# The first stage of a fused SSM, attention and FFN block: low parts by half tiles, spread products in banks of their own, another load order, the last tile's vector on ScalarE

## The chip, the cores and the metric

The kernel runs on one core of a Trainium2 chip. A core has engines that each run their own list of instructions in order and wait for one another by semaphores: TensorE (PE, matrix products into PSUM), VectorE (DVE), ScalarE (ACT), GpSimd (POOL), and SyncE (SP), which here issues the DMA transfers. The metric is the device time of one execution in microseconds, lower is better.

## The reference

The block takes x of 512 tokens by 1024 features. What the edited stage computes is the beginning of it, and a small product that is needed only at the end:

```python
n1 = rmsnorm(h, g_mix[i])                      # x * rsqrt(mean(x*x) + eps) * g_mix
z = n1 @ w_in[i]                               # SSM input, queries, keys and values, gates, merge gates
...
lam = lax.complex(jnp.minimum(a_re, -1e-4), a_im); dt = jnp.exp(log_dt)
a_bar = jnp.exp(lam * dt)                      # modulus rho, angle a_im * dt
...
h = h + gate * (p[i] @ w_ple_proj[i])          # the "embedding" product
```

Between the first and the last lines stand a diagonal state space mixer, an attention with three branches, a merge, and a feed-forward part with a short convolution. They are unchanged.

## The kernel before

Every product is made in three passes of a fast 32-bit format. A number is split in a high part (a copy on ACT that rounds) and a low part (the number less its high part, a subtraction on DVE or POOL); high times high, high times low and low times high are added up in one PSUM bank. `copy` (line 74) is the ACT copy, `tt` (line 53) the subtraction, `mm3` (line 81) the three products. PSUM has eight banks here, in four tags of two: "acc", "s", "t" and "o". A tile that asks for a bank of a tag waits until the reader of the tile that had it before is done. `either()` gives "o" and "acc" in turn.

The order of the first stage is written out by hand for PE, ACT, DVE and POOL (lines 444 to 528): within it each engine runs its instructions as written. Instructions from outside it, and everything after it, are ordered by a planner that simulates the engines' time; it may slip single ones in between (two copies from line 622 and two from line 623 stand in ACT's list in the middle of the stage). `issue_after` keeps some of them behind a named instruction.

The tokens are four tiles of 128 (qt 0 to 3), the features eight slices of 128 (k). The stage does this:

- `embedded(i, qt)`: the product of p with `w_ple_proj`, column half i, token tile qt, two slices by three passes; six products of 512 columns. `embedded_out` copies the bank to memory on ACT, from where SP stores it to DRAM (line 533). The weight halves are loaded in two parts each by `wpload` and split into `wp`.
- `squared` (ACT) sums the squares of a token tile's row form; `rooted` (POOL) makes the reciprocal root of it; `spread` (PE) multiplies it with a scaled identity, so that every partition holds it along the 128 tokens (`rb`, in a bank of tag "s").
- `x_scaled(qt, half)`: DVE multiplies four slices of the transposed x with the column `gmix` and with `rb`, one instruction per slice. `n_high` is the ACT copy of the half, `n_low` the DVE subtraction for the whole tile. They give `n1h` and `n1l`.
- `v_passes(qt, passes)`: three passes of eight products of 280 columns, high by high, low by high, high by low, with the value weights `WV`, in a bank that `either()` gives. The bank that tile 2 gets is the one from which `embedded_out(1, 2)` reads; tile 3's is that of `embedded_out(1, 3)`. `v_high` and `v_low` take gates and values out.
- `u_split(ct, 0)` and `u_split(ct, 1)` are the two parts of the split of the first two weight tiles for the projections.
- `some(n)` runs the next n steps of `angles()` (line 390), small DVE operations on 128x16: steps 1 to 15 end with dt, step 16 is lr = lre * dt, and the following ones make the angles' coarse and fine parts. `some(16)` stands early, `some(50)`, which means all that is left, near the end.

Behind the stage come the projections (`proj`, line 202): 24 products of 512 columns each, with a weight tile that is loaded, copied (high) and subtracted (low). Beside them DVE makes sines and cosines (lines 549 to 578) and POOL makes rho = exp(lr) (line 545), which may start once tile 0's gates are done on POOL; from them come the powers, the input matrix `bb` and its products `z` on DVE, and tables on POOL.

Of the kernel before, what the change touches and what calls it, by code (L numbers as in the profile page):

```python
# [12 lines left out]
AF = mybir.ActivationFunctionType  # L13
# [3 lines left out]
MUL, ADD, SUB = ALU.mult, ALU.add, ALU.subtract  # L17

P = 128
T = 512  # L20
NQ = T // P
D = 1024
KD = D // P
# [21 lines left out]
def hybrid_kernel(ctx: ExitStack, tc: tile.TileContext, A, out):  # L45
    nc = tc.nc
    V, G, S, PE = nc.vector, nc.gpsimd, nc.scalar, nc.tensor

    def dr(name, off, ap):
        t = A[name]  # L50
        return bass.AP(tensor=t.tensor, offset=t.offset + off, ap=ap)

    def tt(o, a, b, op, e=V):
        e.tensor_tensor(o, a, b, op=op)  # L54
# [7 lines left out]
    def stt(o, a, s, b, op0, op1, e=V):  # L62
        e.scalar_tensor_tensor(o, a, s, b, op0=op0, op1=op1)  # L63
# [10 lines left out]
    def copy(o, a):  # L74
        S.activation(o, a, AF.Copy)  # L75
# [24 lines left out]
    def bank(tag, name):  # L100
        return psp.tile([P, 512], F32, tag=tag, name=name, bufs=BANKS[tag])

    def slot(p, tag, shape, dt, name):
        return p.tile(shape, dt, tag=tag, name=name, bufs=1)
# [104 lines left out]
    n1h = slot(pn, "nh", [P, KD, T], F32R, "n1h")  # L209
    n1l = slot(pn, "nl", [P, KD, T], F32R, "n1l")  # L210
# [14 lines left out]
    gmix, gains, dcol, prm, pes, cvp = (cols[:, a:b] for a, b in zip(COLS, COLS[1:]))  # L225
# [7 lines left out]
    xT = slot(cp, "h16", [P, NQ, KD, P], F32, "xT")  # L233
    wv0 = slot(py, "y8", [P, 2, KD, P], F32, "wv0")
    rows = [wv0[:, 1].rearrange("p a b -> p (a b)"), *(px.tile([P, D], F32, name=f"row{qt}") for qt in range(1, NQ))]
    root = px.tile([P, P], F32, name="root")
    ts(root, ident, math.sqrt(D), None, MUL, None, G)
    half = px.tile([P, 1], F32, name="half")
    G.memset(half, -0.5)

    def rowload(qt):
        nc.sync.dma_start(rows[qt], dr("x", qt * P * D, [[D, P], [1, D]]))

    def xload(qt):
        nc.sync.dma_start(xT[:, qt], dr("x_t", qt * P * D, [[D, P], [P, KD], [1, P]]))
# [4 lines left out]
    wpr = slot(pa, "v8", [P, 2, 2, 512], F32, "wpr")  # L250
    wp = [slot(*t, [P, 2, 2, 512], F32R, f"wp{i}") for i, t in enumerate(((pS, "Uc"), (pa, "ptc")))]
    pjd = pud.tile([2, NQ, P, 512], F32, name="pjd")

    def wpload(i, k):
        nc.sync.dma_start(wpr[:, i, k], dr("w_ple_proj", (2 * i + k) * T * P, [[T, P], [1, T]]))
# [2 lines left out]
        nc.sync.dma_start(pin[:, k], dr("p_t", k * T * P, [[T, P], [1, T]]))  # L258
        wpload(0, k)
    nc.sync.dma_start(cols, dr("cols", 0, [[NCOLS, P], [1, NCOLS]]))  # L260
    for qt in range(2):
        rowload(qt)
    for k in range(2):
        wpload(1, k)
    xload(0)
    VV = slot(pa, "v8", [P, NQ, 2, 2, 2, HD], F32R, "VV")
    gates = pa.tile([P, NQ, 24], F32, name="gates")
    WV = slot(pa, "kv", [P, 2, KD, 280], F32R, "WV")
# [13 lines left out]
    def wv(x, i):  # L282
        w0, w, raw = VCOLS[i]
        return WV[:, x, :, w0:w0 + w], raw
# [13 lines left out]
    def v_high(qt):  # L298
        S.activation(gates[:, qt], vps[qt][:, 256:280], AF.Tanh, scale=0.5)
        x, hi, _ = v_parts(qt)  # L300
        copy(hi, x)
        ts(gates[:, qt], gates[:, qt], 0.5, 0.5, MUL, ADD, G)
# [9 lines left out]
    def squared(qt):  # L312
        S.activation(rows[qt], rows[qt], AF.Square, accum_out=ss4[:, qt:qt + 1])

    rbp, rx = {}, {}

    def rooted(qt):

        r = rx[qt] = small("rx")
        ts(r, ss4[:, qt:qt + 1], D * EPS, None, ADD, None, G)  # L320
        tt(r, r, half, ALU.pow, G)

    def spread(qt):
        if not rbp:
            rbp[0] = bank("s", "rb")
        PE.matmul(rbp[0][:, qt * P:(qt + 1) * P], rx[qt].to_broadcast([P, P]), root, start=True, stop=True)

    def x_scaled(qt, half):
        for k in range(4 * half, 4 * half + 4):
            stt(xT[:, qt, k], xT[:, qt, k], gmix[:, k:k + 1], rbp[0][:, qt * P:(qt + 1) * P], MUL, MUL)  # L330

    def n_of(qt, half):
        ks = slice(4 * half, 4 * half + 4)
        return (slice(None), ks, slice(qt * P, qt * P + P)), xT[:, qt, ks]

    def n_high(qt, half):
        o, x = n_of(qt, half)
        copy(n1h[o], x)

    def n_low(qt):  # L340
        o = (slice(None), slice(None), slice(qt * P, qt * P + P))
        tt(n1l[o], xT[:, qt], n1h[o], SUB)

    def normed_tile(qt):
        for half in range(2):
            x_scaled(qt, half)
            n_high(qt, half)

    uw = []

    def u_split(ct, part):
        if not part:
            uw.append([pw.tile([P, KD * P], F32R, name=n, tag=n).rearrange("p (k c) -> p k c", k=KD)
                       for n in ("wh", "wl")])
            copy(uw[ct][0], uraw[ct])
        else:
            tt(uw[ct][1], uraw[ct], uw[ct][0], SUB)
# [67 lines left out]
    def embedded(i, qt, passes=range(3), ks=range(2)):  # L425
        if (i, qt) not in pjb:
            pjb[i, qt] = bank("t" if i and qt < 2 else either(), "pje")
        for k in ks:
            for n in passes:
                PE.matmul(pjb[i, qt], pT[int(n == 1)][:, k, qt * P:(qt + 1) * P], wp[i][:, int(n == 2), k], start=n + k == 0,  # L430
                          stop=n + k == 3)

    def embedded_out(i, qt):
        n = 4 * i + qt
        if n == 0:
            pjs.append(slot(pa, "v4", [P, 2, 512], F32, "pjs0"))
            pjs.append(wv0[:, 1].rearrange("p (k a) b -> p k (a b)", k=2))
        elif n == 4:
            t = slot(pS, "Uc", [P, 4, 512], F32, "pjs2")
            pjs.extend((t[:, :2], t[:, 2:]))  # L440
        pjo[i, qt] = pjs[n // 2][:, n % 2]
        copy(pjo[i, qt], pjb[i, qt])

    with tc.manual_schedule(engines={mybir.EngineType.PE, mybir.EngineType.Activation, mybir.EngineType.DVE,
                                    mybir.EngineType.Pool}):
        warm = bank("s", "warm")
        for _ in range(6):
            PE.matmul(warm[:, :P], ident, root, start=True, stop=True)
        angled = angles()

        def some(n):
            for _ in range(n):
                next(angled, None)

        for k in range(2):
            copy(pT[0][:, k], pin[:, k])
            copy(wp[0][:, 0, k], wpr[:, 0, k])
            tt(pT[1][:, k], pin[:, k], pT[0][:, k], SUB)
            tt(wp[0][:, 1, k], wpr[:, 0, k], wp[0][:, 0, k], SUB)
        squared(0)  # L460
        for k in range(2):
            for n in range(3):
                for qt in range(NQ):
                    embedded(0, qt, (n,), (k,))
        rooted(0)
        some(16)
        squared(1)
        rooted(1)
        for k in range(2):
            copy(wp[1][:, 0, k], wpr[:, 1, k])  # L470
            tt(wp[1][:, 1, k], wpr[:, 1, k], wp[1][:, 0, k], SUB)
        for qt in range(2):
            embedded_out(0, qt)
        embedded(1, 0)
        spread(0)
        embedded(1, 1)
        x_scaled(0, 0)
        n_high(0, 0)
        embedded_out(0, 2)
        x_scaled(0, 1)  # L480
        n_high(0, 1)
        embedded_out(0, 3)
        embedded(1, 2)
        n_low(0)
        copy(*wv(0, 0))
        wv_lo(0)
        copy(*wv(0, 1))
        wv_lo(1)
        embedded(1, 3)
        for qt in range(2):  # L490
            embedded_out(1, qt)
        spread(1)
        v_passes(0, (0, 1))
        squared(2)
        rooted(2)
        normed_tile(1)
        v_passes(0, (2,))
        n_low(1)
        for qt in (2, 3):
            embedded_out(1, qt)  # L500
        spread(2)
        v_passes(1, (0,))
        squared(3)
        rooted(3)
        normed_tile(2)
        v_passes(1, (1, 2))
        n_low(2)
        v_high(0)
        u_split(0, 0)
        exp_at = last(mybir.EngineType.Pool)  # L510
        spread(3)
        v_passes(2, (0,))
        normed_tile(3)
        v_passes(2, (1, 2))
        n_low(3)
        v_high(1)
        v_low(0)
        v_low(1)
        u_split(0, 1)
        some(50)  # L520
        trig_at = last(mybir.EngineType.DVE)
        u_split(1, 0)
        v_passes(3, (0, 1, 2))
        for qt in (2, 3):
            v_high(qt)
            v_low(qt)
        zero_at = last(mybir.EngineType.Activation)
        u_split(1, 1)
# [117 lines left out]
    for lv in range(5):  # L646
        n = 1 << lv
        m = MID + n
        rotate([t[:, :, m:m + n] for t in tab], [t[:, :, MID:m] for t in tab], n, lv, [t[:, :, :n] for t in tabm], G)
    for t, c, sign in zip(tab, (COS, SIN), (1.0, -1.0)):  # L650
        S.activation(t[:, :, 0], c[:, 6], AF.Copy, scale=sign)
        x = t[:, :, HC - 1:HC]
# [28 lines left out]
    for ct in range(4):  # L681
# [3 lines left out]
        for j in range(L):  # L685
            n = L - 1 - j
# [5 lines left out]
    with tc.issue_after(zero_at):  # L692
        for t in (*ZZ[0], *CX[0], *ZZ[1], *CX[1]):
            n = t.shape[1] * t.shape[2] * t.shape[3] * t.shape[4] // 8
# [450 lines left out]
    for hf in range(2):  # L1145
        for c in range(4):
            ks, k4 = slice(2 * c, 2 * c + 2), slice(2 * (c % 2), 2 * (c % 2) + 2)
# [176 lines left out]
    with tc.manual_schedule(engines={mybir.EngineType.PE}):  # L1324
# [73 lines left out]
        for n, c in enumerate(range(NR, NP)):  # L1398
# [5 lines left out]
            x = [u[:, n % NSET] for u in (uh, ul)]  # L1404
# [243 lines left out]
```

## Time and profile before

| | |
|---|---|
| three runs, median (lowest to highest) | 813.5 us (812.31 to 813.54) |
| the profiled execution | 813.89 us, its span 812.1 us |
| PE busy | 794.4 us, 98% |
| DVE, ACT, POOL busy | 520.1, 405.5, 246.6 us |
| first projection starts on PE | 35.26 us |
| sixth projection goes on after its wait | 64.30 us |
| mean granted TensorE clock | 0.997 |

A row of the order of time gives the start, the time until the end of the last merged instruction, the engine, the line, what is written from what, how many instructions are merged, and in brackets the idle time before and what ended it. Helpers put their own line there, so all subtractions are line 54 and all high copies line 75; the tile's name tells them apart: `wp` embedding weights, `pje` embedding product, `xT` and `n1h`, `n1l` the normed input, `WV` value weights, `vps` value products, `wr`, `wh`, `wl` a weight tile and its parts, `pj` a projection, `pjs` copied embedding. PEld are PE's weight loads, which run ahead of the products.

### The profile page before, as it was taken

To read this page: it belongs to the slowest core of one execution; us is meant where nothing else is said; L and a number is where in the kernel's file an instruction comes from. 1 tells how busy PE (TensorE), PEld (TensorE's weight loads), DVE (VectorE), ACT (ScalarE), POOL (GpSimd) and SP (SyncE) were. 2 spreads that over 40 slices of the span, in tenths; PEclk is the share of its full clock that TensorE was granted. 3 is DMA by queue.
4 is the path that set the end of the run, shared out by engine and by line. 5 is a ranking of instruction groups with operands and counts; after the bars stand their busy time and mean duration, and the time that the engine had idled before them with its cause. 6 is when DMAs were issued, how large, how long until landed. Compare 5 with 4: busy or idle time off the path is not lost. (4 is left out here: it accounts for less than half of the span.)

```text
span 812.1 us, 12156 instructions
## 1 busy us (share of the span) xinstructions
PE 794.4 (98%) x4480; PEld 668.9 (82%) x4480; DVE 520.1 (64%) x1102; ACT 405.5 (50%) x747; POOL 246.6 (30%) x281
## 2 busy tenths in 40 slices
PE   8998999999999999999999999999999999999995
PEld 6886888888888888878898888888888888888884
DVE  5898896957777732496444444545544757998754
ACT  6735554357777744344354434443444433584632
POOL 1567130115655544141032333333333200000321
PEclk9999999999999999999999999999999999999998
DMA  9953222243333413244033322333223242525111
GB/s 344 332 191 95 79 66 66 67 113 95 83 76 92 143 52 104 79 154 156 1 116 93 103 89 93 104 105 104 83 99 103 95 165 87 199 72 168 46 53 52
DMA packets 29707, 89.70 MB, mean 110 GB/s; under 512 B 3664, under 2 KB 5840, under 8 KB 29648
## 3 DMA queue, kind: packets, MB, share of 16 engines
q1 hardware_dynamic: 29072, 87.88, 33.0%
q10 hardware_dynamic: 576, 1.05, 0.3%
q8 instruction: 35, 0.57, 0.3%
q14 instruction: 24, 0.20, 0.1%
HBM read 79.48 MB, written 5.24 MB: 104 GB/s over the span
## 5 line engine op out<-in xcount | busy, mean ns | idle before, releaser
L54 POOL TENSOR_TENSOR wl<-wr,wh 128x1024 fp32r<-128x1024 f32 x39 | 93.9, 2409 | 238.7 <-ACT wh L75 238.6
L75 ACT ACTIVATE wh<-wr 128x1024 fp32r<-128x1024 f32 x88 | 93.2, 1059 | 86.6 <-issue 26.4
L54 DVE TENSOR_TENSOR wl<-wr,wh 128x1024 fp32r<-128x1024 f32 x49 | 63.4, 1293 | 52.7 <-ACT wh L75 52.6
L82 PE MATMUL pj<-n1h,wh 128*128 128x512 f32 x224 | 91.0, 406 | 0.6 <-DVE QT L54 0.6
L84 PE MATMUL pj<-n1h,wl 128*128 128x512 f32 x224 | 87.7, 392 | 1.2 <-DVE wl L54 1.2
L83 PE MATMUL pj<-n1l,wh 128*128 128x512 f32 x224 | 87.4, 390 | 0.0
L63 DVE SCALAR_TENSOR_TENSOR cv<-ub,cols,cv 128x511 f32<-128x511 f32 (+1 forms) x44 | 32.9, 748 | 66.2 <-ACT cv L1288 65.5
L83 PE MATMUL ua<-n2l,wh 128*128 128x512 f32 (+1 forms) x176 | 66.9, 380 | 0.2 <-DVE n2l L63 0.2
L82 PE MATMUL ua<-n2h,wh 128*128 128x512 f32 (+1 forms) x176 | 66.9, 380 | 0.0
L84 PE MATMUL ub<-n2h,wl 128*128 128x512 f32 (+1 forms) x176 | 66.8, 379 | 0.0
L83 PE MATMUL ub<-n2l,wh 128*128 128x512 f32 (+1 forms) x176 | 66.8, 379 | 0.0
L82 PE MATMUL ub<-n2h,wh 128*128 128x512 f32 (+1 forms) x176 | 66.8, 379 | 0.0
L84 PE MATMUL ua<-n2h,wl 128*128 128x512 f32 (+1 forms) x176 | 66.8, 379 | 0.0
L84 PEld LDWEIGHTS pj<-n1h,wl 128*128 128x128 f32 x224 | 42.0, 188 | 11.1 <-DVE wl L54 1.6
L82 PEld LDWEIGHTS pj<-n1h,wh 128*128 128x128 f32 x224 | 42.2, 188 | 8.6 <-DVE QT L54 0.8
L60 POOL TENSOR_SCALAR pr<-pr,su,gates 128x512 f32<-128x512 f32 (+1 forms) x64 | 39.1, 620 | 31.2 <-DVE su L1008 28.5
L83 PEld LDWEIGHTS pj<-n1l,wh 128*128 128x128 f32 x224 | 42.2, 188 | 7.1
L54 DVE TENSOR_TENSOR pl<-ptp,ph 128x128 fp32r<-128x128 f32 (+1 forms) x64 | 31.2, 488 | 15.2 <-ACT ph L75 14.9
L54 POOL TENSOR_TENSOR wg1l<-wr,wg1h 128x1024 fp32r<-128x1024 f32 x2 | 5.0, 2490 | 113.4 <-ACT wg1h L75 113.4
L1007 ACT ACTIVATE pr<-pr,nb 128x512 f32<-128x512 f32 (+1 forms) x64 | 35.6, 557 | 7.2 <-DVE nb L1005 7.2
L75 ACT ACTIVATE ph<-ptp 128x128 fp32r<-128x128 f32 (+1 forms) x64 | 27.7, 433 | 23.0 <-PE ptp L1016 22.4
L83 PEld LDWEIGHTS ua<-n2l,wh 128*128 128x128 f32 x176 | 33.1, 188 | 6.6 <-DVE n2l L63 0.4
(476 smaller groups left out, 2058.5 us busy)
## 6 DMA issues: line engine op xcount, KB each, us to landing
wr<-in_w_up_dram SPq DMA_DIRECT2D x44, 512.0 KB, 3.4
wr<-in_w_in_dram SPq DMA_DIRECT2D x28, 512.0 KB, 3.4
b<-in_w_down_dram SPq DMA_DIRECT2D x14, 512.0 KB, 3.7
QQ<-QT SPq DMA_DIRECT2D x16, 256.0 KB, 3.6
wr<-in_w_out_dram SPq DMA_DIRECT2D x8, 512.0 KB, 3.6
wr<-in_w_down_dram SPq DMA_DIRECT2D x8, 512.0 KB, 4.2
wr<-in_w_ple_gate_dram SPq DMA_DIRECT2D x8, 512.0 KB, 3.5
xT<-in_x_t_dram SPq DMA_DIRECT2D x4, 512.0 KB, 9.1
```

The lines of the kernel that those rows point to most:

```text
L54: e.tensor_tensor(o, a, b, op=op)
L60: e.tensor_scalar(o, a, s1, s2, op0=op0, op1=op1)
L63: e.scalar_tensor_tensor(o, a, s, b, op0=op0, op1=op1)
L75: S.activation(o, a, AF.Copy)
L82: PE.matmul(ps, lh, rh, start=start, stop=False)
L83: PE.matmul(ps, lh, rl, start=False, stop=False)
L84: PE.matmul(ps, ll, rh, start=False, stop=stop)
L1007: S.activation(pp, pp, AF.Exp, bias=nb, scale=-1.0, accum_out=su)
```

## The change

The stage's list is written anew; what is computed is the same but for the order of two factors in the last tile.

- `spread` takes a new "s" bank for each tile instead of one bank for four.
- `n_low` makes two subtractions of 512 columns instead of one of 1024.
- For the last tile, ACT multiplies x by `gmix` in place beforehand (`x_multiplied(3)`, eight instructions of 128 columns with a column as scale, between the fourth squaring and the copies of tile 2), and `x_scaled(3, half)` is one DVE product of 512 columns with `rb`.
- The loads go row 0, embedding weight part (1, 0), row 1, x 0, part (1, 1), where before they went row 0, row 1, both parts, x 0.
- The split of part (1, 0) goes ahead of the second squaring; the second half's embedding products go slice by slice, with the first slice of tiles 1 to 3 behind the first spread product.
- The copies out of the embedding's banks go later: (0, 2), (0, 3) behind the value weights' copies, (1, 1) between tile 1's copies, (1, 2), (1, 3) behind tile 2's copies and `v_high(0)`.
- `u_split(0, 0)` goes behind tile 3's copies.
- The early `some(16)` becomes `some(10)` and `some(4)`; so dt and lr are made in `some(50)`.

```diff
@@ loads
-    for qt in range(2):
-        rowload(qt)
-    for k in range(2):
-        wpload(1, k)
+    rowload(0)
+    wpload(1, 0)
+    rowload(1)
     xload(0)
+    wpload(1, 1)
@@ helpers
     def spread(qt):
-        if not rbp:
-            rbp[0] = bank("s", "rb")
-        PE.matmul(rbp[0][:, qt * P:(qt + 1) * P], rx[qt].to_broadcast([P, P]), root, start=True, stop=True)
+        rbp[qt] = bank("s", "rb")
+        PE.matmul(rbp[qt][:, :P], rx[qt].to_broadcast([P, P]), root, start=True, stop=True)
+
+    def x_multiplied(qt):
+        for k in range(KD):
+            S.activation(xT[:, qt, k], xT[:, qt, k], AF.Copy, scale=gmix[:, k:k + 1])
 
     def x_scaled(qt, half):
-        for k in range(4 * half, 4 * half + 4):
-            stt(xT[:, qt, k], xT[:, qt, k], gmix[:, k:k + 1], rbp[0][:, qt * P:(qt + 1) * P], MUL, MUL)
+        ks = range(4 * half, 4 * half + 4)
+        if qt == NQ - 1:
+            x = xT[:, qt, 4 * half:4 * half + 4]
+            tt(x, x, rbp[qt][:, None, :P].to_broadcast([P, 4, P]), MUL)
+            return
+        for k in ks:
+            stt(xT[:, qt, k], xT[:, qt, k], gmix[:, k:k + 1], rbp[qt][:, :P], MUL, MUL)
...
     def n_low(qt):
-        o = (slice(None), slice(None), slice(qt * P, qt * P + P))
-        tt(n1l[o], xT[:, qt], n1h[o], SUB)
...
         for half in range(2):
-            x_scaled(qt, half)
-            n_high(qt, half)
+            tt(n_of(n1l, qt, half), xT[:, qt, 4 * half:4 * half + 4], n_of(n1h, qt, half), SUB)
@@ the list
         squared(0)
+        rooted(0)
         ...
-        rooted(0)
-        some(16)
+        some(10)
+        copy(wp[1][:, 0, 0], wpr[:, 1, 0])
+        tt(wp[1][:, 1, 0], wpr[:, 1, 0], wp[1][:, 0, 0], SUB)
+        some(4)
         squared(1)
         rooted(1)
-        for k in range(2):
-            copy(wp[1][:, 0, k], wpr[:, 1, k])
-            tt(wp[1][:, 1, k], wpr[:, 1, k], wp[1][:, 0, k], SUB)
         for qt in range(2):
             embedded_out(0, qt)
-        embedded(1, 0)
+        embedded(1, 0, ks=(0,))
         spread(0)
-        embedded(1, 1)
+        for qt in range(1, NQ):
+            embedded(1, qt, ks=(0,))
+        copy(wp[1][:, 0, 1], wpr[:, 1, 1])
         x_scaled(0, 0)
         n_high(0, 0)
-        embedded_out(0, 2)
         x_scaled(0, 1)
+        tt(wp[1][:, 1, 1], wpr[:, 1, 1], wp[1][:, 0, 1], SUB)
+        copy(*wv(0, 0))
         n_high(0, 1)
-        embedded_out(0, 3)
-        embedded(1, 2)
         n_low(0)
-        copy(*wv(0, 0))
+        copy(*wv(0, 1))
         wv_lo(0)
-        copy(*wv(0, 1))
         wv_lo(1)
-        embedded(1, 3)
-        for qt in range(2):
-            embedded_out(1, qt)
+        for qt in (2, 3):
+            embedded_out(0, qt)
+        for n in range(3):
+            for qt in range(NQ):
+                embedded(1, qt, (n,), (1,))
+        embedded_out(1, 0)
+        squared(2)
+        rooted(2)
         spread(1)
         v_passes(0, (0, 1))
-        squared(2)
-        rooted(2)
-        normed_tile(1)
+        x_scaled(1, 0)
+        n_high(1, 0)
+        x_scaled(1, 1)
+        embedded_out(1, 1)
+        n_high(1, 1)
         v_passes(0, (2,))
         n_low(1)
-        for qt in (2, 3):
-            embedded_out(1, qt)
+        squared(3)
+        rooted(3)
         spread(2)
         v_passes(1, (0,))
-        squared(3)
-        rooted(3)
-        normed_tile(2)
+        x_multiplied(3)
+        x_scaled(2, 0)
+        n_high(2, 0)
+        x_scaled(2, 1)
+        n_high(2, 1)
         v_passes(1, (1, 2))
         n_low(2)
         v_high(0)
-        u_split(0, 0)
+        for qt in (2, 3):
+            embedded_out(1, qt)
         exp_at = last(mybir.EngineType.Pool)
         spread(3)
         v_passes(2, (0,))
-        normed_tile(3)
+        for half in range(2):
+            x_scaled(3, half)
+            n_high(3, half)
         v_passes(2, (1, 2))
         n_low(3)
+        u_split(0, 0)
         v_high(1)
```

More of the change, by code (lines that the diff above doesn't have):

```diff
@@ L323, in spread, with n_of @@
     def spread(qt):
-        if not rbp:
-            rbp[0] = bank("s", "rb")
-        PE.matmul(rbp[0][:, qt * P:(qt + 1) * P], rx[qt].to_broadcast([P, P]), root, start=True, stop=True)
-    def x_scaled(qt, half):
-        for k in range(4 * half, 4 * half + 4):
-            stt(xT[:, qt, k], xT[:, qt, k], gmix[:, k:k + 1], rbp[0][:, qt * P:(qt + 1) * P], MUL, MUL)
-    def n_of(qt, half):
+        rbp[qt] = bank("s", "rb")
[3 more added lines that the diff above has]
+            S.activation(xT[:, qt, k], xT[:, qt, k], AF.Copy, scale=gmix[:, k:k + 1])
+    def x_scaled(qt, half):
+        ks = range(4 * half, 4 * half + 4)
[5 more added lines that the diff above has]
+            stt(xT[:, qt, k], xT[:, qt, k], gmix[:, k:k + 1], rbp[qt][:, :P], MUL, MUL)
+    def n_of(x, qt, half):
         ks = slice(4 * half, 4 * half + 4)
-        return (slice(None), ks, slice(qt * P, qt * P + P)), xT[:, qt, ks]
+        return x[:, ks, qt * P:qt * P + P]
     def n_high(qt, half):
-        o, x = n_of(qt, half)
-        copy(n1h[o], x)
+        copy(n_of(n1h, qt, half), xT[:, qt, 4 * half:4 * half + 4])
     def n_low(qt):
-        o = (slice(None), slice(None), slice(qt * P, qt * P + P))
-        tt(n1l[o], xT[:, qt], n1h[o], SUB)
-    def normed_tile(qt):
         for half in range(2):
-            x_scaled(qt, half)
-            n_high(qt, half)
+            tt(n_of(n1l, qt, half), xT[:, qt, 4 * half:4 * half + 4], n_of(n1h, qt, half), SUB)
     uw = []
```

## The prediction

> **What bounds the kernel now.** I read the page's engine table first, then the waits of the weight loads over the first 80 us, then the order of time of each engine there. TensorE (PE) is busy for nearly the whole span, so only time in which it stands still can be won:
>
> ```profile
> PE 794.4 (98%) x4480; PEld 668.9 (82%) x4480; DVE 520.1 (64%) x1102; ACT 405.5 (50%) x747; POOL 246.6 (30%) x281
> ```
>
> ```profile
> PEld vps L295 <- DVE n1l L54: 2.0, 3, 0.7
> PEld pj L84 <- DVE wl L54: 1.6, 1, 1.6
> PEld pje L430 <- ACT wp L75: 1.4, 2, 1.3
> PEld vps L295 <- ACT WV L75: 1.2, 1, 1.2
> ...
> PEld rb L326 <- issue: 0.5, 1, 0.5
> ```
>
> Each row gives the time lost, how often, and the longest. All but the second lie in the first stage and make 2.0 + 1.4 + 1.2 + 0.5 = 5.1 us: the most that the edited code can win. The second, 1.6 us, comes later. In order of time on PE:
>
> ```profile
> 10.03 1.07 PE L430 MATMUL pje<-wp,pTh 128*128 128x512 f32 x4
> 11.93 0.50 PE L430 MATMUL pje<-wp,pTh 128*128 128x512 f32 x1 [0.83 <-ACT wp L75]
> ...
> 19.53 1.29 PE L295 MATMUL vps<-WV,n1h 128*128 128x280 f32 x8 [1.02 <-ACT WV L75]
> ...
> 27.38 1.27 PE L295 MATMUL vps<-WV,n1h 128*128 128x280 f32 x8
> ...
> 34.23 1.20 PE L295 MATMUL vps<-WV,n1h 128*128 128x280 f32 x8
> 35.26 0.39 PE L82 MATMUL pj<-n1h,wh 128*128 128x512 f32 x1
> ...
> 62.69 0.39 PE L83 MATMUL pj<-n1l,wh 128*128 128x512 f32 x1
> 64.30 0.50 PE L84 MATMUL pj<-n1h,wl 128*128 128x512 f32 x1 [1.22 <-DVE wl L54]
> ```
>
> The stage ends with the first projection at 35.26. From there PE runs without a stop to 62.69, the sixth projection, and stands until 64.30 for a low weight part that VectorE (DVE) makes late. DVE is then the bound, and its chain hangs on one number, rho, that GpSimd (POOL) computes:
>
> ```profile
> 11.33 0.17 DVE L54 TENSOR_TENSOR lr<-lre,dt 128x16 f32<-128x16 f32 x1
> ...
> 20.89 2.15 DVE L63 SCALAR_TENSOR_TENSOR xT<-xT,cols,rb 128x128 f32<-128x128 f32 x8
> 23.73 1.23 DVE L54 TENSOR_TENSOR n1l<-xT,n1h 128x1024 fp32r<-128x1024 f32 x1 [0.70 <-ACT n1h L75]
> ...
> 33.62 1.21 DVE L54 TENSOR_TENSOR wl<-wr,wh 128x1024 fp32r<-128x1024 f32 x1
> 34.76 0.19 DVE L54 TENSOR_TENSOR th<-cols,dt 128x16 f32<-128x16 f32 x1
> ...
> 37.33 1.21 DVE L54 TENSOR_TENSOR wl<-wr,wh 128x1024 fp32r<-128x1024 f32 x1
> 38.47 0.28 DVE L54 TENSOR_TENSOR ang<-kk,mt 128x128 f32<-128x128 f32 x1
> ...
> 40.36 0.17 DVE L54 TENSOR_TENSOR rho<-rho 128x16 f32<-128x16 f32 x1 [1.41 <-POOL rho L54]
> ...
> 62.49 1.75 DVE L54 TENSOR_TENSOR wl<-wr,wh 128x1024 fp32r<-128x1024 f32 x1
> ```
>
> ```profile
> 29.20 0.28 POOL L60 TENSOR_SCALAR e1x<-lr 128x16 f32<-128x16 f32 x1
> ...
> 37.34 1.32 POOL L58 TENSOR_SCALAR gtFalse<-e1q 128x16 f32<-128x16 f32 x1
> ...
> 40.10 0.22 POOL L54 TENSOR_TENSOR rho<-gtFalse,e1s 128x16 f32<-128x16 f32 x1
> ```
>
> ```profile
> 36.00:50.00 14.00, 14.00 (x64) 11.59 (x62) 12.24 (x54) 8.07 (x14) 5.52 (x15) 1.00 0.53 180
> 50.00:64.00 14.00, 13.08 (x58) 10.51 (x56) 13.45 (x35) 4.64 (x7) 14.00 (x37) 1.00 0.50 166
> ```
>
> (The window's columns: length, then busy time of PE, weight loads, DVE, ACT, POOL.) From 40.36 to 64.24 DVE has no named wait and is 13.45 of 14 us busy in the second stretch. So PE's 64.30 is 40.36 plus 23.9 us of DVE work. After two more short stops PE does not wait again to the end; what stands at 64 us stands in the total.
>
> **The change, part by part.** I rebuilt the stage's order by hand from the durations of such rows; the same working gives 35.3 for the old order.
>
> *Loads.* One 256 KB weight part now lands ahead of the second row tile, the other behind the first x tile. The stage moves 421 GB/s:
>
> ```profile
> 10.00:20.00 10.00, 8.14 (x36) 6.00 (x35) 7.57 (x21) 7.95 (x15) 1.83 (x6) 1.00 1.03 421
> ```
>
> so 256 KB is 0.62 us: the second row tile lands 0.6 later, the first x tile 0.6 earlier. From its issue and the smallest landing time it came at 5.27 + 7.5 = 12.8, so now at 12.15:
>
> ```profile
> 5.27 0.73 SPq L245 DMA_DIRECT2D xT<-in_x_t_dram x1
> ```
>
> ```profile
> DMA to landing us min/median/max: 7.5/9.1/10.2
> ```
>
> Everything from the second V weight on lands as before, and no landing after it sets anything below.
>
> *The early splits.* The copy that PE waits for runs behind two squarings today and behind one afterwards:
>
> ```profile
> 8.91 1.06 ACT L313 ACTIVATE wv<-wv 128x1024 f32<-128x1024 f32 x1 [1.10 <-DMA wv<-in_x_dram]
> ...
> 11.27 1.13 ACT L75 ACTIVATE wp<-wpr 128x512 fp32r<-128x512 f32 x2
> ...
> 23.61 1.07 ACT L75 ACTIVATE pjs<-pje 128x512 f32<-128x512 f32 x2
> 24.56 1.06 ACT L313 ACTIVATE row<-row 128x1024 f32<-128x1024 f32 x1
> ...
> 27.69 0.17 ACT L299 ACTIVATE gates<-vps 128x24 f32<-128x24 f32 x1
> ```
>
> It starts near 10.0, its low part is done near 11.4, and PE, free at 11.0, stands about 0.3 instead of 0.83. The spread product comes near 11.7, the first tile's scaling near 12.2 (landing-bound). DVE then has 2.1 (eight at 0.26), 0.6 (weight low part), 0.7 + 0.7 (halves) and 2.5 (V weights), so the second tile's scaling starts near 18.8 instead of 20.89. On PE the V products start near 17.3 instead of 19.53, when their bank has been emptied: 2.2 us won by here.
>
> *Halves and banks.* Each tile ended with 0.70 us of DVE waiting for the copy of its second half; by halves that is filled at the price of one more instruction start, some 0.08 us. The 0.5 us on rb is a spread product waiting for DVE's reads of the shared bank; it goes. The third and fourth product reuse buffers whose readers are long done. Tile 1's low pass starts near 22.2.
>
> *The last tile's vector.* ACT gets eight 128x128 multiplications by a column. None stands in this trace. Nearest rows:
>
> ```profile
> L148 ACT ACTIVATE xn<-hres,ry 128x512 f32<-128x512 f32 x4 | 2.7, 713 | 0.1
> L1007 ACT ACTIVATE pr<-pr,nb 128x128 f32<-128x128 f32 x16 | 6.3, 397 | 3.3 <-DVE nb L1005 3.3
> ```
>
> A column operand at 128 elements is 0.40 us, at 0.1 overlap 0.30 in a row: 2.4 us in all. Below, 0.20 each: two 512 copies at 11.27 take 1.13, so one 0.62 and a step of 0.51; with 1.06 for 1024 elements an element is 0.86 ns, and 0.51 less 384 of them is 0.18. Above, 0.40 without overlap. I take 2.4, from the row with the same shape. DVE saves two 0.6 steps against 2.1, so 0.9 us. But these eight stand on ACT between the fourth squaring (ending near 22.7) and the copies of tile 2, whose first half DVE has ready near 23.4: they start at 25.1, 1.7 us late. Behind them in ACT's order are the second copy, the gates and values of tile 0, and only then the two copies that empty the embedding's banks, which used to be done at 24.7. The third tile's V products need one of these banks. Sum: 25.1 + 0.54 + 0.54 + (0 to 0.62 for the CT copies of line 623, if they fall here as they do now) + 0.36 + 0.58 = 27.2 to 27.8, against 27.38 today. PE, 2.9 us ahead at 24.5, stands there 2.7 to 3.3 us. From then on it has 48 products at 0.129 us (1.03 per eight, the rows at 34.23 and 35.26): 6.2, and the first projection comes at 33.4 to 34.0, a gain of 1.3 to 1.9 instead of up to 5.1.
>
> The Trainium skill, page "ScalarE: Activation LUTs", section "Rules for kernel authors", speaks against this move: it would leave multiplications on VectorE. By that rule the eight belong on DVE, and the stage would keep about 1 us more. The rows at least agree that the step is dearer on ACT, 0.30 against 0.26 us.
>
> *Moved steps that cost nothing.* The first weight copy for the projections goes behind tile 3's copies, to about 29.3; its low part ends near 32.2 and PE's third product of that projection needs it near 33.9 at the earliest, so 1.7 us of V products hide it. The last embedding stores go to SP when their copies are done:
>
> ```profile
> 29.15 1.28 SPq L533 DMA_DIRECT2D pjd<-pjs  x2
> ...
> 34.90 4.03 SPq L188 DMA_DIRECT2D wr<-in_w_in_dram  x2
> ```
>
> Their copies end near 28.2, still ahead of the present 29.15, and the weight load behind them waits for the first weight split, which comes earlier.
>
> *What DVE and POOL carry on.* DVE ends the first weight split near 32.2 instead of 34.83 (2.6 won). Two operations that were early, dt and lr, now follow it, plus ten as now: the angles start near 36.2 instead of 38.47 (2.2 won). lr, ready at 11.5 before, is ready near 32.5, and POOL's chain to rho can start only then. It took 29.20 to 40.32 = 11.1 us. In it are four operations of 1.0 to 1.3 us like that at 37.34, which begin beside DVE's large subtractions (one at 37.33); of these one stays beside it, so 11.1 less some 2.2, and I take 8.9: rho at 41.4. Bounds: 7.6 (23 operations at 0.33) to 11.1, so rho at 40.1 to 43.6.
>
> The Trainium skill, page "SBUF — State Buffer", section "SBUF: two separate sides", says that a two-input VectorE operation and a GpSimd operation that read SBUF exclude each other for a whole instruction. The pair at 37.33 and 37.34 agrees. By it alone the chain takes the 8.9.
>
> The later operations are ordered by a planner from its own clock. Today it puts rho's first use right behind the second angle operation, where it took rho for ready. With lr so late it cannot; I expect some four microseconds of angle work ahead of it and a DVE stop as now, about 1.4 us. Then DVE keeps its 2.2 us: the sixth weight's low part ends at 64.24 - 2.2 = 62.0. PE arrives there near 61.3 (62.9 less 1.6). So PE passes at about 62.1, and 2.2 us are won at 64.30. I take off 0.1 for the halves' extra instruction starts.
>
> **Sum.** 813.89 (execution of the profile; span 812.1) - 2.1 = 811.8; against the median of the runs, 813.5, which lies 0.4 lower, 811.4.
>
> **Rivals.**
>
> *A, ACT is not late enough to matter.* The column operand costs 0.20, or the CT copies fall elsewhere, and DVE meets no stop for rho. Then the first projection comes at 32.5 and the angles near 35.4, 3.1 us early; without DVE's 1.41 us stop the sixth low part ends up to 4.5 early, and PE, there at 62.9 - 2.8 = 60.1, could win 4.2 at most: between 3.1 and 4.2, say 3.5, so 810.0. For it: the 1.41 us at 40.36 is a stop that a later place would save. Against: the 0.40 us row.
>
> *B, the win is given back before 80 us.* Low parts or the POOL operations behind the angles keep their old times, because the planner puts the sixth split behind more DVE work. With 0.3 us left, 813.2: no change. For it: DVE has no slack from 40 to 64 us.
>
> *C, rho decides, slower.* The planner leaves rho's first use where it is. DVE then stops from about 36.6 until rho, and PE passes at rho + 23.9. With rho at 41.4 this is 65.3, 1.1 us late, 814.6, still within what can be told; from rho at 41.95 it is slower, and at 43.6 it is 3.2 us, 816.7. For it: the order of today. Against: a use planned ahead of its value.
>
> *D, the change doesn't do what it says*: the planner's insertions break up the halves, and the 0.70 waits stay. They are hidden behind PE's stop for the bank, so the time is the forecast's; no case of its own.
>
> **How the numbers follow.** Forecast 0.38, A 0.20, B 0.20, C 0.22. About 0.2% (1.6 us) is what a measurement here can tell from no change, so faster means below 811.9. The forecast, 811.4, is on that side for three quarters of its chance (0.30) and within for 0.08; A faster, 0.20; B the same, 0.20; C half and half, rounded to 0.12 the same and 0.10 slower. Faster 0.50, the same 0.40, slower 0.10. The range reaches from A with a little more, 809.5, to C with rho at 41.4, 814.6; the forecast's own is 810.6 to 812.4.
>
> **What would show it.** PE starts the embedding's second half near 11 and the V products near 17.3; a new wait of about 3 us at the third tile's V products, put down to ACT's copy of the embedding; the first projection at 33.4 to 34.0; POOL's chain starting near 32.5 and ending near 41.4; DVE's stop for rho later in its order; PE's stop at the sixth projection about 0.7 long, ending near 62. The forecast is wrong if PE doesn't wait for the bank, if the column multiplication costs 0.2, or if rho's first use stays behind the second angle operation.

## The result and the profile after

| | kernel before | changed kernel |
|---|---|---|
| median of the runs, us | 813.5 (812.3 to 814.4) | 818.45 (817.86 to 819.05) |
| ratio to before | 1 | 1.0056, 95% interval 1.0044 to 1.0068 |
| profiled execution, span in it | 813.9, 812.1 | 817.9, 816.1 |

The change makes the kernel 0.56% slower, some 4.6 us. The prediction was 811.4 us with a range of 809.5 to 814.6, so even the range missed it.

Waits of the weight loads over the whole span, changed kernel (time lost in us, how often, the longest):

```profile
PEld pj L84 <- DVE wl L54: 2.5, 2, 1.5
PEld vps L295 <- ACT pjs L75: 2.4, 1, 2.4
PEld wbps L752 <- ACT Z L75: 2.2, 1, 2.2
...
PEld ops L1043 <- DVE PTC L54: 2.1, 1, 2.1
```

Only the second row is in the first stage. The three others above 2 us lie behind it, and two of them, the scan's products that wait for ACT's `Z` and the attention's that wait for `PTC`, had no such row before. All rows of this view between 40 and 240 us add up to 7.3 us before and 14.7 us after. In order of time (start, duration, engine; in brackets the idle time before and what ended it), changed kernel:

```profile
17.29 0.92 PE L295 MATMUL vps<-WV,n1h 128*128 128x280 f32 x5 [0.23 <-ACT wv L75]
22.50 2.43 ACT L329 ACTIVATE xT<-xT,cols 128x128 f32<-128x128 f32 x8
...
26.84 1.29 PE L295 MATMUL vps<-WV,n1h 128*128 128x280 f32 x8 [2.17 <-ACT pjs L75]
32.19 0.28 POOL L60 TENSOR_SCALAR e1x<-lr 128x16 f32<-128x16 f32 x1 [0.31 <-DVE th L54]
33.12 0.40 PE L82 MATMUL pj<-n1h,wh 128*128 128x512 f32 x1
...
38.47 0.21 DVE L60 TENSOR_SCALAR qs<-qc 128x128 f32<-128x128 f32 x1
40.83 0.22 POOL L54 TENSOR_TENSOR rho<-gtFalse,e1s 128x16 f32<-128x16 f32 x1
41.09 0.17 DVE L54 TENSOR_TENSOR rho<-rho 128x16 f32<-128x16 f32 x1 [2.41 <-POOL rho L54]
...
56.63 0.50 PE L84 MATMUL pj<-n1h,wl 128*128 128x512 f32 x1 [1.08 <-DVE wl L54]
63.65 1.88 DVE L54 TENSOR_TENSOR wl<-wr,wh 128x1024 fp32r<-128x1024 f32 x1
64.20 0.66 PE L752 MATMUL wbps<-ident,Z 128*128 128x128 f32 x4 [1.81 <-ACT Z L75]
65.59 0.50 PE L84 MATMUL pj<-n1h,wl 128*128 128x512 f32 x1 [0.73 <-DVE wl L54]
...
184.11 5.43 POOL L54 TENSOR_TENSOR wl<-wr,wh 128x1024 fp32r<-128x1024 f32 x2 [25.61 <-ACT wh L75]
184.15 0.38 PE L955 MATMUL pct<-ident,cmps 128*128 128x128 f32 x2
184.63 2.80 DVE L63 SCALAR_TENSOR_TENSOR yg<-sg,yT 128x512 f32<-128x512 f32 x1 [4.21 <-PE pct L955]
184.83 0.98 PE L1016 MATMUL sps<-KK,QQ 128*128 128x512 f32 x4
187.26 0.42 DVE L54 TENSOR_TENSOR PTC<-pct,PTC 128x256 fp32r<-128x256 f32 x1
187.73 0.50 PE L1043 MATMUL ops<-PTC,VC 128*128 128x512 f32 x1 [1.69 <-DVE PTC L54]
234.59 0.46 PE L1016 MATMUL sps<-KK,QQ 128*128 128x256 f32 x2
610.68 0.39 PE L82 MATMUL ub<-n2h,wh 128*128 128x512 f32 x1
```

Rows of the kernel before that answer to these (its first and sixth projection, at 35.26 and 64.30, and its sixth low weight part, at 62.49, stand in the prediction):

```profile
71.08 0.50 PE L82 MATMUL pj<-n1h,wh 128*128 128x512 f32 x1 [0.60 <-DVE QT L54]
...
178.74 2.40 POOL L54 TENSOR_TENSOR wl<-wr,wh 128x1024 fp32r<-128x1024 f32 x1 [21.45 <-ACT wh L75]
181.13 0.38 PE L940 MATMUL pct<-ident,cmps 128*128 128x128 f32 x2
181.61 1.08 DVE L63 SCALAR_TENSOR_TENSOR yg<-sg,yT 128x512 f32<-128x512 f32 x1 [5.06 <-PE pct L940]
182.53 0.41 DVE L54 TENSOR_TENSOR PTC<-pct,PTC 128x256 fp32r<-128x256 f32 x1
183.45 0.97 PE L1001 MATMUL sps<-KK,QQ 128*128 128x512 f32 x4
184.25 0.39 PE L1027 MATMUL ops<-PTC,VC 128*128 128x512 f32 x1
230.66 0.46 PE L1001 MATMUL sps<-KK,QQ 128*128 128x256 f32 x2
606.75 0.39 PE L82 MATMUL ub<-n2h,wh 128*128 128x512 f32 x1
```

Read the same product in both lists. The first projection starts 2.14 us earlier (33.12 against 35.26): the stage does what it was forecast to do. The sixth projection goes on 1.29 us later than before (65.59 against 64.30). The scores' products come 1.38 us later (184.83 against 183.45), 3.93 later at 230.66, and still 3.93 later at 606.75. So 6.07 us are lost between the first projection and 230 us, 3.43 of them by the sixth projection and 2.55 behind the scores' products, and nothing after that.

The first part is lost in two stops. The fifth projection waits 1.08 us for its low weight part (56.63). At the sixth, PE has four of the scan's products in front of the first product with the low part, and they wait 1.81 us for ACT's `Z` (64.20). On DVE the first `z` operations, from 61.11 on, stand ahead of the sixth low weight part, which begins at 63.65; before, the low part began at 62.49 and `z` came behind it.

The stop at 187.73, 1.69 us long, shows how most of the second part is lost. Before, PE transposed the last piece of `cmps` (`pct`) at 181.13, 2.32 us ahead of the scores' products, DVE had put it into `PTC` at 182.9, and PE used it at 184.25. After, the last `pct` products stand at 184.15, only 0.68 us ahead of the scores' products. In both, DVE has one `yg` to do before `PTC`; after the change that `yg` takes 2.80 us instead of 1.08. GpSimd had begun a weight subtraction 0.52 us before it, and a `yg` that has to let it finish would end at 184.11 + 2.40 (one subtraction alone, the row at 178.74) + 1.08 = 187.59; it ended at 187.43. The Trainium skill, page "SBUF — State Buffer", section "SBUF: two separate sides", says that of a two-input VectorE operation and a GpSimd operation that read SBUF, the one that starts first holds the port for its whole length; these rows agree within 0.2 us.

None of this is code that the diff touches. The 5,958 instructions behind the stage on the five queues are the same in both kernels, but the planner put them in another order: of TensorE's 3,929 places 784 hold another instruction, of ACT's 615 110, of VectorE's 961 239.

### The profile page after: what moved, and what is told of

Read it like the earlier page. It is cut to its first block, busy times and chain, and to the rows that moved or that the text cites. A ratio compares the mean times of both kernels' runs of the same rounds, so it can differ in the third digit from the quotient of the medians.

```text
span 816.1 us, 12158 instructions
## 1 busy us (share of the span) xinstructions
PE 795.1 (97%) x4480; PEld 668.4 (82%) x4480; DVE 522.7 (64%) x1100; ACT 407.3 (50%) x755; POOL 246.6 (30%) x281
## 5 line engine op out<-in xcount | busy, mean ns | idle before, releaser
L75 ACT ACTIVATE ph<-ptp 128x128 fp32r<-128x128 f32 (+1 forms) x64 | 27.8, 434 | 25.5 <-PE ptp L1031 24.8
```

## The experiments

Theory O: the loss is the order that the planner wrote behind the stage. Rival S: the stage's own new timing (ACT late, lr and rho late) makes the loss. To part the two, the order behind the stage was pinned: each instruction there gets an issue-order edge, without any wait, to the one before it on its engine in a recorded order.

```diff
+    for ks in later_order().values():        # one list of positions per engine
+        for k0, k1 in zip(ks, ks[1:]):
+            tc.add_manual_dep(later[k1], later[k0].name,
+                              mybir.DependencyInfo(mybir.DependencyClass.NoSync, mybir.DependencyReason.DATA),
+                              reason="later_order")
```

All experiments compute everything that the kernel before computes. Ratios are to the kernel before on the same chip, whose median was 813.7 to 813.8 us; a ratio rests on all executions and can differ from the quotient of the two medians by 0.0006.

| experiment | stage | order behind it | us | ratio, 95% interval |
|---|---|---|---|---|
| `old_stage_new_order` | before | the changed kernel's | 819.3 | 1.0064 (1.0049 to 1.0079) |
| `new_stage_old_order` | changed | the one before | 814.7 | 1.0013 (1.0002 to 1.0024) |
| `new_stage_lr_early` | changed, lr early | planner's | 815.4 | 1.0019 (1.0009 to 1.0029) |
| `new_stage_lr_early_old_order` | changed, lr early | the one before | 812.9 | 0.9986 (0.9976 to 0.9995) |
| `lr_late_alone` | before, lr late | the one before | 817.7 | 1.0047 (1.0032 to 1.0062) |
| `lr_late_free` | before, lr late | planner's | 814.6 | 1.0016 (1.0006 to 1.0025) |
| `x_back_only` | changed, vector back on VectorE | planner's | 812.1 | 0.9986 (0.9976 to 0.9995) |
| `new_stage_x_back_order` | changed | that of `x_back_only` | 813.0 | 0.9986 (0.9975 to 0.9997) |
| `halves_banks` | before, with halves and banks | the one before | 812.9 | 0.9987 (0.9978 to 0.9997) |
| `no_move` | changed, vector back, lr early, bank copies ahead | the one before | 812.9 | 0.9989 (0.9980 to 0.9999) |
| `no_move_free` | as `no_move` | planner's | 810.1 | 0.9949 (0.9934 to 0.9963) |
| `old_stage_no_move_order` | before | that of `no_move_free` | 813.3 | 0.9998 (0.9988 to 1.0008) |

### The stage, or the order behind it

`old_stage_new_order` leaves the first stage untouched and pins the changed kernel's order behind it.

> The first stage as before, everything behind it in the order that the changed kernel has there. Theory O: the order alone loses what the changed kernel loses behind the first projection, 6.0 us (4.0 in the span plus the 2.1 won), less up to 0.8 because rho comes earlier: 818 to 819.5 us. Theory R: rho is early again, so 813.5 us.

Its waits of the weight loads:

```profile
PEld ops L1029 <- DVE PTC L54: 2.1, 1, 2.1
...
PEld wbps L738 <- ACT Z L75: 2.0, 1, 2.0
```

819.3 us: the order alone costs the whole loss and a little more. The stops for `Z` and `PTC` are there again, and PE passes the sixth projection at 65.99; only the fifth does not wait. Even `yg` is long again, 2.79 us, beside the same two weight subtractions on GpSimd.

`new_stage_old_order` is the other half: the changed stage, and behind it the order of before.

> The changed first stage as it is, but everything behind the stage is issued on every engine in the order that the kernel before has there. Theory O (the planner's new order behind the stage costs the time): the 2.1 us won at the first projection stay, less what rho takes: with the old order VectorE waits for rho right behind the second angle operation until about 41.1, 0.7 us later than before, so the sixth projection goes on near 65.0 and the time is 813.5 + 0.7 = 814.2 us, and the losses near 140 to 190 us are gone. Theory R (the late rho costs it all, whatever the order): 818 us as the changed kernel.

In order of time, and the window of 28 to 30 us (length, then busy time of PE, weight loads, DVE, ACT, POOL, then the granted clock of TensorE, the DMA share and GB/s):

```profile
26.75 2.23 PE L295 MATMUL vps<-WV,n1h 128*128 128x280 f32 x8 [2.18 <-ACT pjs L75]
34.59 0.40 PE L82 MATMUL pj<-n1h,wh 128*128 128x512 f32 x1
41.20 0.17 DVE L54 TENSOR_TENSOR rho<-rho 128x16 f32<-128x16 f32 x1 [4.35 <-POOL rho L54]
65.14 0.50 PE L84 MATMUL pj<-n1h,wl 128*128 128x512 f32 x1 [2.69 <-DVE wl L54]
```

```profile
28.00:30.00 2.00, 2.00 (x11) 2.00 (x10) 1.63 (x3) 2.00 (x5) 0.06 (x1) 0.50 1.08 385
```

814.7, close to no change, as expected of O. (The pinning itself shows no cost: `old_stage_no_move_order`, below, is pinned too and takes 0.9998 of the time before.) This is rival C of the prediction to the letter: rho's first use left where it was, rho at 41.2, PE passing the sixth projection at 41.20 + 23.9 = 65.1, and 814.6 forecast for it. One thing was new: the first projection came at 34.59, 1.5 us later than in the changed kernel, because behind the stop of 2.18 us the granted clock was 0.50 and eight products took 2.23 us instead of 1.29.

### What a late lr costs

Four runs change only how many of the small operations come early, so that lr is early or late.

```diff
-        some(4)      # changed stage: lr early
+        some(6)
-        some(16)     # old stage: lr late
+        some(14)
```

> The changed first stage with dt and lr made early (some(6)), everything behind it in the order of the kernel before. If order and rho together are the loss, this one shows the whole gain: first projection near 33.1, no wait for rho, VectorE's chain 3.6 us earlier, the sixth projection without its stop, 810.0 us. If something in the stage itself costs time that shows later (banks, stores, loads), it stays above 812 us.

812.9 instead of 810.0. rho came at 37.4 and PE's stop at the sixth projection fell to 1.62 us, but the clock was at 0.50 again from 28 to 30 us and the first projection at 34.99.

> The changed kernel, but some(4) is some(6), so dt and lr are made early as before; the planner orders the rest anew. Theory R: rho is ready near 37, VectorE does not wait for it, and 3 to 3.5 us are won against before: 810 to 810.5 us. Theory O: another order, whose losses nobody can foretell, 811 to 818 us.

815.4, slower than the same stage under the old order by 2.5 us. Here 25 of TensorE's places differ from before, and a stop of 2.55 us for DVE's `QT` stands at 73.23, with a granted clock of 0.50 from 74 to 76 us behind it. The planner's own order costs time here too, though it is nearly the old one.

> The kernel before with some(14) for some(16), so only dt and lr are made late; everything behind the stage in the order of the kernel before. Theory R (rho is on the path): lr near 35.2, POOL's chain from there 8.7 to 9 us, rho near 44, VectorE stops until then and the sixth projection goes on at 44 + 23.9 = 68: 3.7 us slower, 817.3 us. Theory O alone (only the order counts): no change, 813.6 us.

The old stage with lr late, under the old order, and below it the same stage with the planner free:

```profile
43.49 0.17 DVE L54 TENSOR_TENSOR rho<-rho 128x16 f32<-128x16 f32 x1 [5.00 <-POOL rho L54]
...
68.30 0.79 PE L84 MATMUL pj<-n1h,wl 128*128 128x512 f32 x1 [4.03 <-DVE wl L54]
```

```profile
45.70 0.17 DVE L54 TENSOR_TENSOR rho<-rho 128x16 f32<-128x16 f32 x1 [1.74 <-POOL rho L54]
```

> The kernel before with dt and lr late (14 operations ahead of them instead of 16, the rest behind), the planner free: TensorE and ACT keep their order to the last instruction, VectorE's rho use moves ten operations back. With the old order pinned this stage took 817.7. Theory (late lr costs through rho's place only, and the planner mends most of it): VectorE's stop for rho 5.0 - 3.3 = 1.7 us, the sixth projection 3 us earlier than pinned: 814 to 815.5. Rival (late lr is dear whatever the order): 817 to 818.5.

A late lr costs 4 us when the order stays (817.7) and about 1 us when the planner may answer (814.6): it moves rho's use ten operations back, VectorE's stop falls from 5.00 to 1.74 us, and the orders on TensorE and ACT stay the same to the last instruction. So a late lr by itself doesn't bring the costly order.

### Which edit turns the order

`x_back_only` is the changed kernel with the last edit of the title undone:

```diff
-        if qt == NQ - 1:
-            x = xT[:, qt, 4 * half:4 * half + 4]
-            tt(x, x, rbp[qt][:, None, :P].to_broadcast([P, 4, P]), MUL)
-            return
...
-        x_multiplied(3)
```

> The changed kernel with one edit undone: the last tile's vector goes back into VectorE's scaling (eight scalar-tensor-tensor operations, none on ACT); dt and lr stay late, and the planner is free. It then writes TensorE's and ACT's orders behind the stage exactly as before the change; on VectorE it puts rho's first use some ten operations later than before. Theory (the loss is the order written behind the stage, and this edit is what tips it): no stop at the third tile's V products, first projection at 31 to 32, rho near 41, its stop on VectorE under 1.5 us, sixth projection passed near 62, no stop of 1.7 us at 187: 811 to 812.5 us. Rival (the late lr costs what is lost): 816 to 818.5.

```profile
26.33 1.30 PE L295 MATMUL vps<-WV,n1h 128*128 128x280 f32 x8 [1.23 <-ACT pjs L75]
32.61 0.40 PE L82 MATMUL pj<-n1h,wh 128*128 128x512 f32 x1
...
61.80 0.50 PE L84 MATMUL pj<-n1h,wl 128*128 128x512 f32 x1 [1.32 <-DVE wl L54]
69.46 0.50 PE L82 MATMUL pj<-n1h,wh 128*128 128x512 f32 x1 [0.67 <-DVE QT L54]
605.11 0.39 PE L82 MATMUL ub<-n2h,wh 128*128 128x512 f32 x1
```

812.1 us, as expected: without this one edit the changed kernel takes 5.7 us less, by the two ratios (1.0056 and 0.9986), and is a little faster than the kernel before. The path missed its expectation in places. Of the stop at the third tile's V products 1.23 us stayed, since the bank copies still stand behind tile 2's copies on ACT; the first projection came at 32.61 instead of 31 to 32; and rho was used at 42.61 behind a stop of 1.75 us, where 41 and under 1.5 were expected. PE passes the sixth projection 2.50 us earlier than before (61.80 against 64.30); 1.62 of these are left at 69.46 against 71.08, because PE then waits 0.60 us for ACT's `Z`, which it didn't before, and again for DVE's `QT`, and 1.64 are there at 605.11 against 606.75. So with TensorE's order unchanged a shift does last to the end, but from 71 us, not from 64.

`new_stage_x_back_order` keeps the changed stage, vector on ACT and all, and pins the order of `x_back_only` behind it. This is the kernel that the prediction had in mind: rho's use later on VectorE, all else in the old order.

> The changed stage as it is, with the order behind it pinned to the one that the planner writes for the kernel with the vector back on VectorE: the old order on TensorE and ACT, rho's first use some ten operations later on VectorE. This is the kernel that the prediction took the changed one to be. By the prediction's steps: rho near 41, VectorE's stop for it about 1 instead of the 4.35 us that the changed stage had under the old order, the sixth projection passed some 2.5 to 3 us earlier than there: 811.5 to 812.3, or up to 813.5 where the clock falls behind the stop at the third tile. Rival (the changed stage itself loses): above 815.

```profile
27.42 1.61 PE L295 MATMUL vps<-WV,n1h 128*128 128x280 f32 x8 [2.19 <-ACT pjs L75]
35.23 0.39 PE L82 MATMUL pj<-n1h,wh 128*128 128x512 f32 x1
41.79 1.22 DVE L54 TENSOR_TENSOR wl<-wr,wh 128x1024 fp32r<-128x1024 f32 x1 [2.98 <-ACT wh L75]
43.34 0.17 DVE L54 TENSOR_TENSOR rho<-rho 128x16 f32<-128x16 f32 x1
```

```profile
28.00:30.00 2.00, 2.00 (x12) 2.00 (x11) 1.53 (x3) 2.00 (x5) 0.00 (x0) 0.55 1.11 310
```

813.0 us: VectorE has no stop for rho, because it stands 2.98 us shortly ahead of it, for a weight copy on ACT (41.79); PE has no stop at the sixth projection and passes it at 62.89. From the third tile's first V product to the first projection it took 7.81 us (35.23 - 27.42), against 6.28 in the changed kernel (33.12 - 26.84): 1.5 us went to the lower clock. Three of its ten executions, with a mean granted clock of 0.997, took 811.0 to 811.3 us; the other seven, at 0.994 to 0.996, the profiled one among them, took 812.7 to 813.6. That the clock did not fall here in those three is likely, but not shown.

So the edit that moved the last vector to ACT costs little as work: under one and the same order the two stages lie 0.9 us apart in the medians, and their ratios to before are equal (0.9986). It costs 5 us because, together with the rest of the stage, it tips the planner into another order. It takes both it and the late lr: with lr early only 25 of TensorE's places differ, with the vector back none. The old stage with the vector on ACT, and with lr late too, keeps TensorE's order as well (read from the planner's programs, which were not run). Why the planner's clock tips just there stays open.

### The parts, and a better version

`halves_banks` adds only the low parts by halves and the separate banks to the kernel before.

> The kernel before with only two parts of the change: low parts by halves and a bank for each spread product; the order behind the stage as before. By VectorE's rows: three waits of 0.7 us filled for 0.08 each and the 0.5 us wait on the bank gone, so the first projection near 33.5, rho some 0.5 us earlier, the sixth projection 0.5 to 1.5 us earlier: 812.1 to 813.1 us.

```profile
63.79 0.50 PE L84 MATMUL pj<-n1h,wl 128*128 128x512 f32 x1 [2.40 <-DVE wl L54]
```

812.9 us, 0.13% faster. The first projection comes at 33.57, 1.7 us earlier, and 2.40 us are then spent waiting at the sixth: the gain at the stage's end is given back to VectorE, as rival B thought, here under the old order.

`no_move` takes the vector back to VectorE, makes lr early and puts the bank copies right behind the fourth squaring, so that nothing on ACT stands ahead of them; `no_move_free` is the same with the planner free.

> The changed stage without the vector on ScalarE (the last tile is scaled on VectorE like the others), the copies out of the last two embedding banks right behind the fourth squaring, dt and lr early, everything behind in the order of the kernel before. Theory S (ScalarE's eight multiplications make the 2.4 us stop of TensorE and the half clock after it): no stop at the third tile's products, full clock, first projection near 31, rho near 36.5, the sixth projection about 4 us earlier, 809.5 to 810.5 us. If the stop has another cause, it stays and the time is that of the same order with the vector moved, 812.9 us.

> The same stage, with the planner free to order what is behind it. Theory O: it finds another order, whose loss may be anything from 0 to 6 us against the order of before: 810 to 816 us. If the order only suffers from the late lr, it is as fast as with the old order, within 0.5 us.

First `no_move`, then `no_move_free`:

```profile
27.47 0.29 POOL L822 COPY W2d<-W 128x128 f32<-128x128 f32 x1 [1.14 <-DMA W<-in_cmp_wk_dram]
31.38 0.40 PE L82 MATMUL pj<-n1h,wh 128*128 128x512 f32 x1
38.79 0.17 DVE L54 TENSOR_TENSOR rho<-rho 128x16 f32<-128x16 f32 x1 [3.21 <-POOL rho L54]
63.61 0.80 PE L84 MATMUL pj<-n1h,wl 128*128 128x512 f32 x1 [4.03 <-DVE wl L54]
```

```profile
30.84 0.40 PE L82 MATMUL pj<-n1h,wh 128*128 128x512 f32 x1
36.41 0.17 DVE L54 TENSOR_TENSOR rho<-rho 128x16 f32<-128x16 f32 x1 [1.27 <-POOL rho L54]
```

Both win 4 us at the first projection. Under the old order PE then waits 4.03 us at the sixth, and `no_move` missed its forecast: the old order has GpSimd copy `W2d` in the middle of its chain to rho, and with lr this early the copy waits 1.14 us for its load. Behind the stop the granted clock was 0.50 from 62 to 68 us, which took more of the gain. With the planner free the copy stands later, rho is used at 36.41 instead of 38.79, there is no stop at the sixth projection, and the kernel takes 810.1 us, 0.5% faster than before: the best version that was run. TensorE's order is the old one in it, and only 12 of VectorE's places differ.

> The kernel before, with the order behind the stage pinned to the one of the best version (the changed stage without the move and with lr early). That order differs from the old one in 12 places on VectorE, 7 on GpSimd and 5 of the DMA queue, none on TensorE and ACT. Theory (that version's gain over the same stage under the old order, 2.9 us, comes from GpSimd's chain to rho no longer standing behind a copy that waits for a load; in the old stage that load has landed before the chain begins): within 0.8 us of before, 812.9 to 814.4. Rival (the order is the better one for any stage): 810.5 to 811.5.

813.3, no change, as expected: that order is no better in itself. It fits that stage.

## Why the prediction was wrong

Point by point, by its own steps:

- *The early splits*, V products near 17.3: 17.29.
- *The last tile's vector*, eight multiplications in 2.4 us, from the row of the same shape: 2.43. The stop that follows was forecast at 2.7 to 3.3 us and was 2.17, and the first projection at 33.4 to 34.0 was at 33.12. Right in kind, 0.3 us too late. (The terms of the sum add up to 27.1 to 27.7, not 27.2 to 27.8.) The prediction has no term for the clock that can fall behind this stop; in the changed kernel's profile it did not fall.
- *lr near 32.5 and rho at 41.4*: GpSimd's chain began at 32.19 and took 8.86 us (8.9 forecast) to 41.05. The working counts four long operations in the old chain; there are three, the fourth, at 27.95, stands ahead of it. One stayed, as forecast.
- *rho's first use goes behind some four microseconds of angle work*: it did (the row at 41.09 follows the one at 38.47). The stop there was 2.41 us where 1.4 was taken; this term was mis-sized by 1.0.
- *PE passes the sixth projection at about 62.1, and what stands at 64 us stands in the total*: **this is the step that failed.** PE passed it at 65.59. The step took for granted that the planner would move rho's use and leave every other order as it was. The order that it wrote instead put `z` ahead of the sixth low weight part and the scan's products ahead of PE's use of it, and later made the stop for `PTC`; it cost 5.5 us with the old stage in front of it (819.3 against 813.8). Under the order that the step assumed, `new_stage_x_back_order` took 813.0 us, and 811.0 to 811.3 in three executions. That these three come near the forecast 811.4 does not confirm its path: in the profiled execution VectorE's stop was 2.98 us and for ACT, not 1.4 and for rho, and PE passed the sixth projection at 62.89. The second half of the step failed by itself as well: with TensorE's old order, `x_back_only` kept only 1.62 of the 2.50 us that it had won at the sixth projection.

The rivals shared this step. A, B and C each asked what VectorE and rho would do to the sixth projection; C was right for its own condition (814.6 forecast, 814.7 measured in `new_stage_old_order`). B came nearest to what decided: its condition, that the planner puts the sixth split behind more VectorE work, was met (63.65), but B let it cost no more than the win, and had nothing for TensorE's order or for what follows behind 80 us. The range ended where C ended, because every bound in it came from the edited code and rho.

The remark that by the rule of the Trainium skill (page "ScalarE: Activation LUTs", section "Rules for kernel authors") the eight multiplications belong on VectorE, worth 1 us, pointed to the right edit by luck, for another reason. The two profiles put the edit's own work, the stage of `x_back_only` against the changed one, at 0.5 us at the first projection (32.61 against 33.12), where the clock does not fall, and most of the 5.7 us came by way of the planner.

## What to carry to other kernels

Where a planner orders the work behind an edit, the written order is part of the change: compare the two orders, engine by engine, before summing durations, and if they differ far from the edit, add the stops of the new order or pin the old one. A gain at the end of a stage is worth what the next late producer leaves of it; here that was VectorE's chain behind rho, and 1.7 to 3.9 us won at the first projection came down to some 1 us (`halves_banks`, `x_back_only`, `no_move`). Only `no_move_free`, with rho early as well and no stop at the sixth projection, kept some 4 of its 4.4. Undo one edit at a time with the planner left free: the edit that costs most may cost little as work.

## What the runs showed of the hardware

- After a stop of TensorE of 2.2 us at the third tile's V products the granted clock fell in four of the five profiles that have this stop, to 0.50 or 0.55 in a window of 28 to 30 us in three of them and to 0.50 from 30 to 32 in the fourth (`new_stage_lr_early`), and it cost some 1.5 us (the rows of `new_stage_old_order` and `new_stage_x_back_order`). In the fifth, the changed kernel's, the stop of 2.17 us was followed by eight products in 1.29 us at a clock of 1.00, and behind 1.23 us in `x_back_only` they took 1.30. The stop of 2.69 us at 65.14 in `new_stage_old_order` left the clock at 1.00. The Trainium skill, page "TensorE: Matmul & The Clock Gate", section "What's actually happening", has the clock watched over a free-running window of about 3.4 us, which fits that the same stop sometimes costs and sometimes doesn't; it puts the fall at one idle window, and here 2.2 us of idling was enough. Behind 4.03 us in `no_move` and `lr_late_alone` the next product took 0.80 and 0.79 us instead of 0.50.
- GpSimd's chain to rho took 8.9 us in the changed kernel, 11.1 in the kernel before and 12.7 in `no_move`. The operations of the chain are the same; the longer two also have the copy of `W2d` and one or two more operations on gates between them. Of the rest, 1.14 us in `no_move` is the wait for a load, and single operations took 1.0 to 1.3 us instead of 0.2 to 0.4 where they began beside a VectorE subtraction (37.34 beside 37.33 in the prediction's rows).
